# Both layers' embedding projections in the norm of the first block, none at the end of differential attention

## The chip, the cores and the metric

One NeuronCore of a Trainium2 chip runs one program. The metric is the time of one execution on the device, in microseconds (us). The engines are TensorE (PE, matrix products and transposes), VectorE (DVE), ScalarE (ACT), GpSimd (POOL) and SyncE (SP, which here only issues DMAs). Each runs its own instructions in its own order and waits on semaphores for the others.

## What is computed

One sequence of 256 tokens of width 1024 goes through a first block and then through two layers of a second block. All arithmetic is float32. Cut to what matters:

```
x  = layer_norm(ALPHA*x + g1 * token_mixer(modulate(x)))      # first block
ff = (silu(h @ w_gate) * (h @ w_up)) @ w_down
x  = layer_norm(ALPHA*x + g2 * ff, ln2_g, ln2_b)              # the norm that ends it
for i in (0, 1):                                              # second block
    h = h + mixer_i(rms_norm(h))          # 0: gated linear attention, 1: differential attention
    h = h + swiglu_2(rms_norm(h))
    gate = sigmoid(rms_norm(h, ple_norm[i]) @ ple_w_gate[i])
    h = h + gate * (p[i] @ ple_w_proj[i])                     # p[i]: 256 x 256, an input
```

The embedding projection of layer i is p[i] @ ple_w_proj[i], 256 x 256 times 256 x 1024. It depends on nothing but inputs, so it may be computed anywhere before the last line of its layer.

## The kernel before

The 256 tokens are two tiles (t = 0, 1) of 128. A product in float32 is made of three: weights and activations are each split into a rounded part (wh, xh, hh, ph) and a rest (wl, xl, hl, pl), and mm3 (L157) issues wh times xh, wl times xh and wh times xl. Weights are loaded by SP into staging tiles (st, 11 buffers) and split by gran (L141): ScalarE casts wh (L150), VectorE subtracts to get wl (L151), into tiles of wp with five buffers each. Activations are split the same way after they have been transposed on TensorE.

PSUM has eight banks: four under the tag mm (the results of projections and some transposes), four under acc (accumulators of the long products and other transposes). The program is written in Tile: the Python code issues instructions in program order, a scheduler then orders each engine's instructions, earlier code first and later code where an engine would stand, and adds the semaphores. A tile whose tag has n buffers waits until an earlier user of a buffer is done.

Block 1 ends with ffn (L803) and norm_pair (L794): norm_tile (L773) adds the residual on VectorE, squares on ScalarE (jk, L785), takes the power on GpSimd, scales x on ScalarE (L791), transposes it on TensorE and makes hT (L197), xh (L177) and xl (L178) of it, half a tile at a time. Behind it comes gla (L922), whose first projection (proj, L224) reads w_gla in four granules of 256 rows and, at its end, calls later: normed (L798) on GpSimd, two operations of 128 x 1024 for each tile (L799, L800).

ple(i, wk) (L870) is the embedding projection. For each t it loads p[i] into pr (two buffers), transposes it into an mm bank, and splits it into ph (L880) and pl (L881), each of one buffer; it splits two rows of weights; then for each t it issues 12 matmuls into two mm banks and copies them to pp (L892). Before the change ple(0) stands ahead of norm_pair in block 1, and ple(1) near the end of diff (L1144), with steps of the attention handed to it as between.

In diff the projections of q, k and v are made in six parts (parts, L1251) of 512 columns. Steps of the attention stand between their granules: heads (sc_, L1187) makes the scores of two heads for one t, the maxima (L1196), the exponentials (L1202) and the difference of both softmaxes (L1209); heads_t (at_, L1213) transposes it; out_of (L1224) multiplies by v and norms; out_t (L1245) transposes and splits the result into gt. out_rows(kb) (L1285) splits a row of the output weights and issues 12 matmuls for it; finish (L238) issues the last four rows.

The rest of what the change touches: Arow and e of attn_p (L636) in block 1 share the tag Ae with two buffers in pool b1a; bcp has two buffers under bc, which bcast (L275) fills with l1g, l1b, l2g and l2b. bias2 (L318) holds a row of biases for g2_part (L728).

Of the kernel before, what the change touches and what calls it, by code (L numbers as in the profile page):

```python
# [10 lines left out]
F32 = mybir.dt.float32  # L11
# [8 lines left out]
D = 1024  # L20
DFF = 2816
P = 128
# [60 lines left out]
def body(ctx, tc, d, out, dbg=None):  # L83
    nc = tc.nc
    V, A, T, G, Y = nc.vector, nc.scalar, nc.tensor, nc.gpsimd, nc.sync
# [7 lines left out]
    bcp = ctx.enter_context(tc.tile_pool(name="bcp", bufs=2))  # L93
# [8 lines left out]
    def mm():  # L102
        return psp.tile([P, 512], F32, name="mmb", tag="mm")
# [185 lines left out]
    def block1(adp):  # L289
        with ExitStack() as es:  # L290
# [24 lines left out]

            bias = adp.tile([P, 512], F32, name="bias")
            G.memset(bias, 0.0)
            bias2 = adp.tile([P, D], F32, name="bias2")  # L318
            G.memset(bias2, 0.0)
            wada = d["w_ada"][0]  # L320

# [27 lines left out]
                r = rstd_of(ss, 8, 1.0 / 64, EPS)  # L349
                V.tensor_tensor(v3(y, 64), v3(y, 64), head_b(r, 8, 64), op=OP.mult)  # L350

            Arow = [at_.tile([P, 1024], F32, name=f"A{t}", tag="Ae", bufs=2) for t in range(2)]
            vv = [at_.tile([P, 64], F32, name=f"vv{t}") for t in range(2)]
            u = [ap_.tile([P, 512], F32, name=f"u{t}", tag="ug", bufs=4) for t in range(2)]
            gb = [ap_.tile([P, 512], F32, name=f"gb{t}", tag="ug", bufs=4) for t in range(2)]
# [280 lines left out]
            def attn_p(t, g):  # L636
                nk = (t + 1) * P
                ts_ = slice(t * P, (t + 1) * P)
                if g == 0:
                    l8s[t] = sm.tile([P, 8], F32, name="l8", tag="l8")  # L640
                e = at_.tile([P, 4, nk], F32, name="e", tag="Ae" if t else "e0", bufs=2)
                bs = [ac(), ac()]
                for i in range(2):
                    for par, b in enumerate(bs):
                        T.matmul(b[:, i * S:i * S + nk], qT[par * 64:par * 64 + 64, 2 * g + i, ts_],
                                 kT[par * 64:par * 64 + 64, :nk], start=True, stop=False)
                    for b in bs:
                        T.matmul(b[:, i * S:i * S + nk], identr, masks[t][:, :nk], start=False, stop=True)
                for par, b in enumerate(bs):
                    bv = v3(b, S)[:, :, :nk]  # L650
                    mx = sm.tile([P, 2], F32, name="mx", tag="mx")
                    V.reduce_max(mx, bv, axis=AX.X)
                    V.tensor_scalar(mx, mx, -0.125, None, op0=OP.mult)
                    for i in range(2):
                        h = 2 * (2 * g + i) + par
                        A.activation(e[:, 2 * par + i, :], bv[:, i, :], AF.Exp, bias=mx[:, i:i + 1],
                                     scale=0.125, accum_out=l8s[t][:, h:h + 1])
                return e
# [67 lines left out]
            l1b = bcast(d["ln1_b"][0], D)  # L726

            def g2_part(hf):  # L728
                Y.dma_start(bias2[0:1, hf * 512:hf * 512 + 512], d["b_ada"][0:1, 5 * D + hf * 512:5 * D + hf * 512 + 512])
                bk, part, _ = ada_mm(ada_stage(((5 * D + hf * 512, 512),)), ac)  # L730
                V.tensor_add(part, bk, bias2[:, hf * 512:hf * 512 + 512])
                return bk, part

            def g2_row(hf, bk, part):
# [11 lines left out]
            hx = XT()  # L746
# [6 lines left out]
        with tc.tile_pool(name="f1", bufs=1) as wk:  # L753
            acc = ffn(gate_up([(d["w_gate"][0], 0), (d["w_up"][0], 0)]), d["w_down"][0], hx, None, wk,
                      {1: lambda: normed(V, l1g, l1b, 0), 3: lambda: normed(V, l1g, l1b, 1)})
            hx = XT()
            l2g = bcast(d["ln2_g"][0], D)
            l2b = bcast(d["ln2_b"][0], D)
            pp = ple(0, wk)
            gb2 = rsp.tile([P, 32], F32, name="gb2", tag="gb2", bufs=1)  # L760
            V.tensor_mul(gb2[:, 0:8], L2G, MIXG[0])
            V.tensor_mul(gb2[:, 8:16], L2B, MIXG[0])
            norm_pair(acc, g2row, gb2[:, 0:8], gb2[:, 8:16], hx, wk, ac)
            rs = [rsp.tile([P, 1], F32, name="rsx", tag="rsx") for t in range(2)]

            def later(junk):
                for t in range(2):
                    normed(G, l2g, l2b, t)
                for t in range(2):
                    rms_of(t, junk, rs[t])  # L770
            return hx, rs, later, pp

    def norm_tile(t, acc, grow, scale, shift, xt, wk, bank):  # L773
        jk = wk.tile([P, D], F32, name="jk", tag="jk", bufs=1)
# [19 lines left out]
    def norm_pair(*args):  # L794
        for t in range(2):
            norm_tile(t, *args)
# [70 lines left out]
        return r  # L867


    def ple(i, wk, between={}):  # L870
        pt = []
        for t in range(2):
            pr = wk.tile([P, 256], F32, name="pr", tag="pr", bufs=2)
            Y.dma_start(pr, d["p_2"][i, 0, t * P:(t + 1) * P, :])
            tp = mm()
            for k in range(2):
                tr(tp[:, k * P:(k + 1) * P], pr[:, k * P:(k + 1) * P])
            h = wk.tile([P, 2, P], F32R, name="ph", tag="ph", bufs=1)
            l = wk.tile([P, 2, P], F32R, name="pl", tag="pl", bufs=1)
            A.copy(h, v3(tp[:, :256], P))  # L880
            V.tensor_sub(l, v3(tp[:, :256], P), h.bitcast(F32))  # L881
            pt.append((h, l))
        pp = [ppp.tile([P, D], F32, name=f"pp{t}", bufs=1) for t in range(2)]
        gr = [row_gran(d["ple_w_proj_2"][i], k) for k in range(2)]
        for t in range(2):
            bk = [mm(), mm()]
            for k in range(2):
                wh, wl = gr[k]
                mm3(bk, pt[t][0][:, k, :], pt[t][1][:, k, :], [wh[:, :512], wh[:, 512:]], [wl[:, :512], wl[:, 512:]],
                    k == 0, k == 1)  # L890
            for n in range(2):
                A.copy(pp[t][:, n * 512:(n + 1) * 512], bk[n])  # L892
            for f in between.get(t, ()):
                f()
        return pp

    def ple_gate(i, xt, rs, pp, wk):
# [18 lines left out]

    ppp = ctx.enter_context(tc.tile_pool(name="ppp", bufs=1))
    with tc.tile_pool(name="adp", bufs=1) as adp:
        hx, rs, later, pp = block1(adp)


    def gla(xt, rs, wk):  # L922
# [185 lines left out]
    def tail_layer(i, acc, pp, nxt):  # L1108
        with tc.tile_pool(name=f"tl{i}", bufs=1) as wk:
            junk = wk.tile([P, D], F32, name="junk")  # L1110
            hx = XT()
            for t in range(2):
                residual_rms(t, acc, FFNG[i], hx, ac)
            rs = [rms_of(t, junk) for t in range(2)]
            for t in range(2):
                dump(f"mix{i}", x[t], t)
            acc = ffn(gate_up([(d["ffn_w_in_2"][i], 0), (d["ffn_w_in_2"][i], DFF)]), d["ffn_w_out_2"][i], hx, rs, wk,
                      {3: lambda: diff_consts(wk)} if nxt else {})
            hx = XT()
            for t in range(2):  # L1120
                residual_rms(t, acc, PLEG[i], hx, mm)
            rs = [rms_of(t, junk) for t in range(2)]
            for t in range(2):
                dump(f"ffn{i}", x[t], t)
            fin = ple_gate(i, hx, rs, pp, wk)
            if nxt:
                hx = XT()
                for t in range(2):
                    for n in range(2):
                        fin(t, n)  # L1130
                        hx.put_gain(t, n, blocks_t(x[t][:, n * 512:n * 512 + 512], ac), MIXG[1])
                for t in range(2):
                    dump(f"ple{i}", x[t], t)
                return hx, [rms_of(t, junk) for t in range(2)]
            for t in range(2):
                for n in range(2):
                    hs = slice(n * 512, n * 512 + 512)
                    fin(t, n)
                    Y.dma_start(out[0, t * P:(t + 1) * P, hs], x[t][:, hs])

    hx, rs = tail_layer(0, acc, pp, True)


    def diff(xt, rs, wk):  # L1144
# [121 lines left out]
        def at_(hp, t):  # L1266
            heads_t(hp, t, es[hp, t])

        def c(f, *a):
            return lambda: f(*a)  # L1270
# [6 lines left out]
                                2: [c(at_, 1, 0)], 3: [c(at_, 1, 1)]})  # L1277
        parts(1536, qk("k", 1), {0: [c(out_of, 0, 0)], 1: [c(qk_t, "q", 1, 0), c(out_of, 0, 1)], 2: [c(qk_t, "q", 1, 1)]})
        parts(2560, v_of(1), {0: [c(out_t, 0, 0)], 1: [c(qk_t, "k", 1, 0), c(out_t, 0, 1)],
                              2: [c(qk_t, "k", 1, 1)], 3: [c(sc_, 2, 0), c(sc_, 2, 1)]})  # L1280
        pp = ple(1, wk, {0: [c(at_, 2, 0), c(sc_, 3, 0)], 1: [c(at_, 2, 1), c(sc_, 3, 1)]})
        acc = accs(mm)
        wo, late = d["diff_w_out_2"][0], []

        def out_rows(kb):  # L1285
            wh, wl = row_gran(wo, kb)
            for t in range(2):
                both(acc[t], *gt(kb, t), wh, wl, kb == 0, False)

        at_(3, 0)  # L1290
        out_rows(0)
        at_(3, 1)
        out_of(1, 0)
        out_rows(1)
        out_of(1, 1)
        out_rows(2)
        out_t(1, 0)
        out_rows(3)
        out_t(1, 1)
        for kb in range(4, 8):  # L1300
            late.append((lambda t, kb=kb: gt(kb, t), *row_gran(wo, kb), False))
        finish(acc, late)
        return acc, pp

    ctx3 = tc.tile_pool(name="difw", bufs=1)
    wk = ctx3.__enter__()
    acc, pp = diff(hx, rs, wk)
    ctx3.__exit__(None, None, None)
    tail_layer(1, acc, pp, False)


_INS = ["x", "c", "w_ada", "b_ada", "w_in", "conv_w", "attn_norm_g", "conv_norm_g", "w_out", "ln1_g", "ln1_b",
# [23 lines left out]
```

## Time and profile before

| | us |
|---|---|
| median of 3 runs | 1066.44 (1065.1 to 1066.7) |
| the profiled execution | 1059.51 |
| its span, first to last instruction | 1057.7 |
| TensorE busy in the span | 1014.9 |
| VectorE busy | 631.4 |
| ScalarE busy | 560.5 |
| GpSimd busy | 56.3 |

The profile is one execution. All times below are us from the start of its span. A busy engine is one with an instruction under way; TensorE's matmuls overlap one another, so their spacing says more than their durations. The granted clock is a share of full speed: 1.00 is 2.4 GHz, and 0.5 is 1.2 GHz; a stretch with a value between has some of each. The mean over the span is 0.991.

### The profile page before, as it was taken

The page shows a single profiled execution, that of the slowest core. Times are in us where ns is not written, and L with a number is a line of the kernel's source. Part 1 is how long each engine was busy: PE and PEld are TensorE (multiplying, and loading weights), DVE is VectorE, ACT ScalarE, POOL GpSimd, SP SyncE. Part 2 cuts the span into 40 slices and gives each one's busy share as a digit, 9 for nine tenths or more (in the row PEclk, how much of TensorE's full clock was granted, in tenths as well). Part 3 has the DMA queues.
Part 4 walks back from the last instruction along what each step waited for, and adds up shares of the span by engine and source line. Part 5 has one row for each costly group of instructions (what it writes and reads, how often), then busy time and mean ns, then how long its engine had stood idle before and what let it go on. Part 6 is the DMA issues. An engine that isn't in the chain of part 4 may idle for free.

```text
span 1057.7 us, 13558 instructions
## 1 busy us (share of the span) xinstructions
PE 1014.9 (96%) x4883; PEld 810.6 (77%) x4883; DVE 631.4 (60%) x1021; ACT 560.5 (53%) x910; POOL 56.3 (5%) x47
## 2 busy tenths in 40 slices
PE   6899998999999999999999999999998999999998
PEld 3676675888888778887788888887777778888886
DVE  2378468555556466567554547578786655555654
ACT  2355448444454568465544446566857554444643
POOL 0000100000000130000000000004020100000000
PEclk9999999999999999999999999999999999999999
DMA  9958577866666155255666657535433365666601
GB/s 301 386 200 308 202 276 263 273 195 185 193 196 198 50 175 186 81 166 156 194 190 180 192 187 266 147 127 171 135 120 111 124 187 191 186 190 187 239 1 40
DMA packets 131640, 194.48 MB, mean 184 GB/s; under 512 B 10562, under 2 KB 93390, under 8 KB 131572
## 3 DMA queue, kind: packets, MB, share of 16 engines
q1 hardware_dynamic: 130792, 193.21, 57.0%
q8 instruction: 38, 0.62, 0.2%
q10 hardware_dynamic: 780, 0.40, 0.1%
q14 instruction: 30, 0.25, 0.1%
HBM read 192.53 MB, written 1.05 MB: 183 GB/s over the span
## 4 chain that ended last, share of the span: by engine, by line
PE 79%; DVE 8%; ACT 6%; DMA 2%; issue 2%; POOL 1%; SPq 0%; ACTq 0%; DVEq 0%; POOLq 0%
PE mmb L162 16%; PE mmb L159 16%; PE mmb L160 16%; PE acb L162 7%; PE acb L159 7%; PE acb L160 7%; DVE wl L151 2%; PE mmb L124 2%; ACT wh L150 1%; PE acb L124 1%; POOL rs L272 1%; ACT e L1202 1%; DMA st<-in_w_ada_dram 1%; PE mmb L333 1%; PE acb L333 1%
## 5 line engine op out<-in xcount | busy, mean ns | idle before, releaser
L151 DVE TENSOR_TENSOR wl<-st,wh 128x1024 fp32r<-128x1024 f32 (+4 forms) x292 | 350.9, 1207 | 240.1 <-ACT wh L150 237.2
L150 ACT CAST wh<-st 128x1024 fp32r<-128x1024 f32 (+4 forms) x292 | 300.6, 1038 | 280.6 <-PE mmb L162 143.6
L159 PE MATMUL mmb<-wh,xh 128*128 128x512 f32 (+4 forms) x888 | 353.4, 399 | 6.3 <-ACT xh L386 4.5
L160 PE MATMUL mmb<-wl,xh 128*128 128x512 f32 (+4 forms) x888 | 346.8, 391 | 2.1 <-DVE wl L151 2.1
L162 PE MATMUL mmb<-wh,xl 128*128 128x512 f32 (+4 forms) x888 | 342.8, 391 | 6.0 <-DVE xl L178 4.7
L159 PEld LDWEIGHTS mmb<-wh,xh 128*128 128x128 f32 x888 | 169.1, 191 | 44.7 <-ACT xh L386 6.3
L162 PEld LDWEIGHTS mmb<-wh,xl 128*128 128x128 f32 x888 | 169.1, 190 | 44.5 <-DVE xl L178 6.3
L160 PEld LDWEIGHTS mmb<-wl,xh 128*128 128x128 f32 x888 | 169.3, 191 | 33.3 <-DVE wl L151 2.8
L159 PE MATMUL acb<-wh,hh 128*128 128x512 f32 x216 | 84.0, 389 | 0.0
L160 PE MATMUL acb<-wl,hh 128*128 128x512 f32 x216 | 84.0, 389 | 0.0
L162 PE MATMUL acb<-wh,hl 128*128 128x512 f32 x216 | 66.6, 389 | 0.0
L159 PEld LDWEIGHTS acb<-wh,hh 128*128 128x128 f32 x216 | 40.6, 188 | 8.4
L162 PEld LDWEIGHTS acb<-wh,hl 128*128 128x128 f32 x216 | 40.5, 188 | 8.4
L160 PEld LDWEIGHTS acb<-wl,hh 128*128 128x128 f32 x216 | 40.5, 188 | 8.4
L866 POOL TENSOR_TENSOR rsx<-rsx,mhalf 128x1 f32<-128x1 f32 x12 | 10.2, 851 | 468.2 <-DVE rsx L865 468.2
L272 POOL TENSOR_TENSOR rs<-rs,mhalf 128x8 f32<-128x8 f32 (+1 forms) x14 | 20.0, 1433 | 241.1 <-DVE rs L271 241.1
L836 ACT ACTIVATE sg<-mmb,rsx 128x256 f32<-128x256 f32 x44 | 20.7, 474 | 22.2 <-PE mmb L162 20.4
L151 DVE TENSOR_TENSOR wxl<-st,wxh 128x1024 fp32r<-128x1024 f32 x22 | 26.7, 1219 | 3.1 <-ACT wxh L150 3.1
L837 DVE SCALAR_TENSOR_TENSOR sg<-mmb,rsx,sg 128x256 f32<-128x256 f32 x44 | 20.8, 480 | 11.1 <-ACT sg L836 11.1
L150 ACT CAST wxh<-st 128x1024 fp32r<-128x1024 f32 x22 | 22.7, 1052 | 5.1 <-PE acb L162 3.0
L124 PE MATMUL mmb<-ident,sg 128*128 128x128 f32 x132 | 21.1, 275 | 2.7 <-DVE sg L837 2.1
L843 DVE TENSOR_TENSOR hl<-mmb,hh 128x512 fp32r<-128x512 f32 x33 | 22.6, 685 | 1.8 <-ACT hh L842 1.8
(311 smaller groups left out, 1062.7 us busy)
## 6 DMA issues: line engine op xcount, KB each, us to landing
st<-in_ffn_w_in_dram SPq DMA_DIRECT2D x176, 256.0 KB
st<-in_ffn_w_out_dram SPq DMA_DIRECT2D x44, 512.0 KB
st<-in_w_ada_dram SPq DMA_DIRECT2D x32, 512.0 KB
st<-in_diff_w_in_dram SPq DMA_DIRECT2D x24, 512.0 KB
st<-in_w_gate_dram SPq DMA_DIRECT2D x44, 256.0 KB
st<-in_w_up_dram SPq DMA_DIRECT2D x44, 256.0 KB
st<-in_w_down_dram SPq DMA_DIRECT2D x22, 512.0 KB
st<-in_w_ada_dram SPq DMA_DIRECT2D x32, 256.0 KB
```

Of the source, the lines that this page charges most:

```text
L124: T.transpose(o, i, ident)
L150: A.copy(h[:, :n], src)
L151: V.tensor_sub(l[:, :n], src, h[:, :n].bitcast(F32))
L159: T.matmul(p_, xh, wh, start=start, stop=False)
L160: T.matmul(p_, xh, wl, start=False, stop=False)
L162: T.matmul(p_, xl, wh, start=False, stop=stop)
L272: G.tensor_tensor(r[:, :n], r[:, :n], mhalf[:, :n], op=OP.pow)
L333: T.matmul(bk[32 * j:32 * j + 32, :n], cB[:, kb, :], sts[kb // k][:, kb % k * n:kb % k * n + n], start=kb < 4, stop=kb >= 4)
L836: A.activation(sg, ps[t][:, 0:256], AF.Silu, scale=rs[t])
L837: V.scalar_tensor_tensor(sg, ps[t][:, 256:512], rs[t], sg, op0=OP.mult, op1=OP.mult)
L843: V.tensor_sub(hl, tv, hh.bitcast(F32))
L1202: A.activation(es_[:, i, :], b[:, i * S:(i + 1) * S], AF.Exp, bias=mx[:, i:i + 1], scale=rh[:, i:i + 1], accum_out=L[t][:, s, 2 * hp + i:2 ...
```

## The change

ple(1) is called in block 1, right after norm_pair, and the results of both layers are kept to their use: pp has four tiles where it had two. In diff nothing stands in the place of ple(1); the steps of the attention that it carried are written out between the output rows, in a new order, and sc(2, 0) moves one granule up. The parameter between of ple goes. In SBUF, bias2 is halved (the first half of g2's bias uses bias), and Arow and the second tile's e take their two buffers from bcp under the tag bc, where the broadcast rows of the layer norms are.

```diff
-            bias2 = adp.tile([P, D], F32, name="bias2")
+            bias2 = adp.tile([P, 512], F32, name="bias2")
...
-            Arow = [at_.tile([P, 1024], F32, name=f"A{t}", tag="Ae", bufs=2) for t in range(2)]
+            Arow = [bcp.tile([P, 1024], F32, name=f"A{t}", tag="bc") for t in range(2)]
...
-                e = at_.tile([P, 4, nk], F32, name="e", tag="Ae" if t else "e0", bufs=2)
+                e = bcp.tile([P, 4, nk], F32, name="e", tag="bc") if t else at_.tile([P, 4, nk], F32, name="e", tag="e0", bufs=2)
...
-                Y.dma_start(bias2[0:1, hf * 512:hf * 512 + 512], d["b_ada"][0:1, 5 * D + hf * 512:5 * D + hf * 512 + 512])
+                Y.dma_start(bias2[0:1, :] if hf else bias[0:1, :], d["b_ada"][0:1, 5 * D + hf * 512:5 * D + hf * 512 + 512])
                 bk, part, _ = ada_mm(ada_stage(((5 * D + hf * 512, 512),)), ac)
-                V.tensor_add(part, bk, bias2[:, hf * 512:hf * 512 + 512])
+                V.tensor_add(part, bk, bias2 if hf else bias)
...
-            pp = ple(0, wk)
+            pps = [ple(0, wk)]
...
             norm_pair(acc, g2row, gb2[:, 0:8], gb2[:, 8:16], hx, wk, ac)
+            pps.append(ple(1, wk))
...
-    def ple(i, wk, between={}):
+    def ple(i, wk):
+        bank = mm
...
-        pp = [ppp.tile([P, D], F32, name=f"pp{t}", bufs=1) for t in range(2)]
+        pp = [ppp.tile([P, D], F32, name=f"pp{i}{t}", bufs=1) for t in range(2)]
...
-            for f in between.get(t, ()):
-                f()
...
         parts(2560, v_of(1), {0: [c(out_t, 0, 0)], 1: [c(qk_t, "k", 1, 0), c(out_t, 0, 1)],
-                              2: [c(qk_t, "k", 1, 1)], 3: [c(sc_, 2, 0), c(sc_, 2, 1)]})
-        pp = ple(1, wk, {0: [c(at_, 2, 0), c(sc_, 3, 0)], 1: [c(at_, 2, 1), c(sc_, 3, 1)]})
+                              2: [c(qk_t, "k", 1, 1), c(sc_, 2, 0)], 3: [c(sc_, 2, 1)]})
...
+        at_(2, 0)
+        sc_(3, 0)
+        out_rows(0)
+        at_(2, 1)
+        sc_(3, 1)
+        out_rows(1)
         at_(3, 0)
-        out_rows(0)
+        out_rows(2)
+        out_of(1, 0)
         at_(3, 1)
-        out_of(1, 0)
-        out_rows(1)
         out_of(1, 1)
-        out_rows(2)
+        out_rows(3)
         out_t(1, 0)
-        out_rows(3)
         out_t(1, 1)
...
-    tail_layer(1, acc, pp, False)
+    tail_layer(1, acc, pps[1], False)
```

## Rows read from the trace of the kernel before

**Rows 1.** Page, part 1: busy us, share of the span, instructions.
```profile
PE 1014.9 (96%) x4883; PEld 810.6 (77%) x4883; DVE 631.4 (60%) x1021; ACT 560.5 (53%) x910; POOL 56.3 (5%) x47
```

**Rows 2.** Page, part 4: the chain that ended last, shares by engine.
```profile
PE 79%; DVE 8%; ACT 6%; DMA 2%; issue 2%; POOL 1%; SPq 0%; ACTq 0%; DVEq 0%; POOLq 0%
```

**Rows 3.** Stretches, differential attention: length, busy PE, PEld, DVE, ACT, POOL, clock, DMA share, GB/s.
```profile
743.00:765.00 22.00, 20.50 (x103) 15.45 (x103) 16.64 (x43) 18.92 (x46) 0.00 (x0) 1.00 0.32 100
...
795.00:800.00 5.00, 3.00 (x17) 2.12 (x15) 4.55 (x13) 3.55 (x13) 0.00 (x0) 0.95 0.72 222
800.00:803.30 3.30, 3.30 (x13) 2.47 (x11) 1.59 (x6) 2.89 (x9) 0.00 (x0) 0.56 0.00 0
```

**Rows 4.** Order of time, PE, ple(1): start, us, instruction, [idle before, releaser].
```profile
795.56 0.66 PE L124 MATMUL mmb<-ident,pr 128*128 128x128 f32 x4
798.22 0.50 PE L159 MATMUL mmb<-wh,ph 128*128 128x512 f32 x1 [2.00 <-ACT ph L880]
798.55 0.39 PE L160 MATMUL mmb<-wl,ph 128*128 128x512 f32 x1
798.78 0.40 PE L159 MATMUL mmb<-wh,ph 128*128 128x512 f32 x1
...
800.29 0.63 PE L160 MATMUL mmb<-wl,ph 128*128 128x512 f32 x1
800.72 0.63 PE L159 MATMUL mmb<-wh,ph 128*128 128x512 f32 x1
```

**Rows 5.** Order of time, PE, the norm that ends block 1.
```profile
365.45 0.62 PE L162 MATMUL mmb<-wh,pl 128*128 128x512 f32 x2
...
367.52 0.46 PE L159 MATMUL mmb<-wh,xh 128*128 128x416 f32 x1 [0.68 <-ACT xh L177]
...
369.50 0.71 PE L162 MATMUL mmb<-wh,xl 128*128 128x416 f32 x1 [1.33 <-DVE xl L178]
...
372.43 0.55 PE L160 MATMUL mmb<-wl,xh 128*128 128x416 f32 x1
...
373.20 0.35 PE L160 MATMUL mmb<-wl,xh 128*128 128x416 f32 x1
373.39 0.35 PE L162 MATMUL mmb<-wh,xl 128*128 128x416 f32 x1
...
380.94 0.46 PE L162 MATMUL mmb<-wh,xl 128*128 128x416 f32 x1 [1.90 <-DVE xl L178]
```

**Rows 6.** Stretches, the norm: columns as in the first such group.
```profile
370.00:374.00 4.00, 4.00 (x16) 3.84 (x15) 2.79 (x3) 3.55 (x7) 1.67 (x1) 0.64 0.02 6
```

**Rows 7.** Groups of instructions, 793.5 to 827: line, operation, count, busy us, mean ns.
```profile
L892 ACT COPY pp<-mmb 128x512 f32<-128x512 f32 x4 | 2.1, 594 | 0.0
...
L881 DVE TENSOR_TENSOR pl<-mmb,ph 128x256 fp32r<-128x256 f32 x2 | 0.8, 420 | 0.8 <-PE mmb L162 0.8
```

**Rows 8.** Order of time, ACT, the norm.
```profile
372.65 0.90 ACT L150 CAST wh<-st 128x832 fp32r<-128x832 f32 x1
```

**Rows 9.** Tile xl, 350 to 385 (ns min/median/max), and POOL in order of time.
```profile
L178 DVE TENSOR_TENSOR xl<-hT,xh x4: 691/1815/2857, 367.5 to 378.0; 128x512 fp32r<-128x512 f32 x4
...
377.36 2.97 POOL L800 TENSOR_TENSOR x<-x,bc 128x1024 f32<-128x1024 f32 x1
```

**Rows 10.** Tile bc: count, ns min/median/max, first and last start in us.
```profile
L277 SPq DMA_DIRECT2D bc<-in_ln_b_dram x2: 465/539/613, 95.9 to 197.5; - x2
L799 DVE TENSOR_TENSOR x<-x,bc x2: 1217/1221/1225, 166.1 to 173.7; 128x1024 f32<-128x1024 f32 x2
```

**Rows 11.** Order of time, PE, the last transposes of block 1's e.
```profile
121.19 1.09 PE L124 MATMUL acb<-ident,e 128*128 128x128 f32 x8
```

**Rows 12.** Stretches, block 1: columns as in the first such group.
```profile
60.00:66.00 6.00, 6.00 (x32) 5.32 (x32) 5.50 (x20) 5.34 (x9) 0.00 (x0) 1.00 0.86 302
...
156.00:162.00 6.00, 6.00 (x35) 4.27 (x37) 3.87 (x12) 2.73 (x5) 1.00 (x1) 1.00 0.00 1
```

**Rows 13.** Waits of SP, 330 to 390: total us, times, longest.
```profile
SPq L130 <- DVE wl L151: 48.8, 11, 24.9
```

More of the change, by code (lines that the diff above doesn't have):

```diff
@@ L770, in later @@
                     rms_of(t, junk, rs[t])
-            return hx, rs, later, pp
+            return hx, rs, later, pps
     def norm_tile(t, acc, grow, scale, shift, xt, wk, bank):
@@ L874, in ple @@
             Y.dma_start(pr, d["p_2"][i, 0, t * P:(t + 1) * P, :])
-            tp = mm()
+            tp = bank()
             for k in range(2):
@@ L882, in ple @@
             pt.append((h, l))
-        pp = [ppp.tile([P, D], F32, name=f"pp{t}", bufs=1) for t in range(2)]
+        pp = [ppp.tile([P, D], F32, name=f"pp{i}{t}", bufs=1) for t in range(2)]
         gr = [row_gran(d["ple_w_proj_2"][i], k) for k in range(2)]
         for t in range(2):
-            bk = [mm(), mm()]
+            bk = [bank(), bank()]
             for k in range(2):
@@ L918, in body @@
     with tc.tile_pool(name="adp", bufs=1) as adp:
-        hx, rs, later, pp = block1(adp)
+        hx, rs, later, pps = block1(adp)
     def gla(xt, rs, wk):
@@ L1139, in tail_layer @@
                     Y.dma_start(out[0, t * P:(t + 1) * P, hs], x[t][:, hs])
-    hx, rs = tail_layer(0, acc, pp, True)
+    hx, rs = tail_layer(0, acc, pps[0], True)
     def diff(xt, rs, wk):
@@ L1302, in diff @@
         finish(acc, late)
-        return acc, pp
+        return acc
     ctx3 = tc.tile_pool(name="difw", bufs=1)
     wk = ctx3.__enter__()
-    acc, pp = diff(hx, rs, wk)
+    acc = diff(hx, rs, wk)
     ctx3.__exit__(None, None, None)
-    tail_layer(1, acc, pp, False)
+    tail_layer(1, acc, pps[1], False)
 _INS = ["x", "c", "w_ada", "b_ada", "w_in", "conv_w", "attn_norm_g", "conv_norm_g", "w_out", "ln1_g", "ln1_b",
```

## The prediction

> **What bounds the kernel now.** I read the page first: TensorE is busy 96% of the span [rows 1], and 79% of the chain that ended last is TensorE's [rows 2]. Matrix work sets the time, so a change pays only where TensorE waits or runs at its low clock. No instruction on TensorE is added or dropped here: one projection of 24 matmuls, ple(1), moves from the end of differential attention to the norm that ends block 1. What counts is how much waiting it leaves behind and how much it fills.
>
> So I read two stretches by the view of stretches, then by the order of time. At the end of differential attention, in 795 to 800 us TensorE is busy 3.00 of 5 us and in 800 to 803.3 its granted clock is 0.56 [rows 3]. The order of time names the cause: ple(1)'s first matmul waited 2.00 us for ph, ScalarE's cast, and some 2 us later the same matmuls start 0.43 us apart (800.29, 800.72) instead of 0.23 (798.55, 798.78) [rows 4]: the 1.2 GHz level after a gap in 2.4 GHz work. The projection meant as cover for the softmax stands in ScalarE's queue between the exponentials and is itself late.
>
> In the norm, with ple(0) already there, TensorE waits 0.68 us for xh, 1.33 us for xl and later 1.90 us for the last xl [rows 5], and from 370 to 374 the clock is 0.64 [rows 6], which costs 4 x 0.36 = 1.4 us. Together 5.3 us could be filled.
>
> **What leaves differential attention.** 24 matmuls x 0.23 = 5.5 us and four transposes, some 0.6 us (0.66 for the row of four) [rows 4]: 6.1 us of TensorE. With them go the 2.00 us wait for ph [rows 4] and the low clock, 3.3 x 0.44 = 1.5 us [rows 3]. That is 9.6 us. Off ScalarE go four pp copies (2.1 us) and two ph casts, off VectorE two pl (0.8 us) [rows 7], besides the weight splits of two rows.
>
> What comes back is softmax without that cover. Out_rows(0) to (3), 12 matmuls or 2.8 us each, now stand one behind each sc/at step, and sc(2,0) starts inside the last projection. The same chain of four head steps runs in the first half under other projections: from 743 to 765 TensorE is idle 22.00 - 20.50 = 1.5 us [rows 3]. I take 1.5 us, because that row has the same instructions on ScalarE and VectorE. The bounds are 0 (all covered) and 1.5 + 2.0 + 1.5 = 5.0 us (the wait and the low clock return elsewhere). At the very end out_t(1,0) has out_of(1,1) and one out_rows in front of it where it had out_of(1,1) and one and a half; that small loss is in the 1.5. Gain: 9.6 - 1.5 = 8.1 us, between 4.6 and 9.6.
>
> **What the norm pays.** It receives the 6.1 us. If all 5.3 us of waits were filled, it would pay 0.8 us. I don't expect that, for three reasons. First, the scheduler gives each engine what comes first in the program, and later work only where an engine would stand. ple(1) is written behind norm_pair. In the norm ScalarE is the full engine: the first instruction on it that belongs to work behind the norm is a weight cast at 372.65 [rows 8]. Second, ph has one buffer, held until ple(0)'s last matmul (365.45 + 0.62) [rows 5], so ple(1)'s ph can't be cast in the earlier quiet time; I put it in the place of that weight cast, near 372.7. Third, wh has five buffers. Before, ple(0)'s two rows and three granules of gla's first projection were split ahead; now it is four ple rows and one granule. Eleven gla matmuls started from 367.52 to 372.43 [rows 5]; with one granule and only the first token tile ready there are six. The five that are missing cost 5 x 0.19 = 1.0 us (spacing 373.20 to 373.39 [rows 5]).
>
> So the waits of 0.68 and 1.33 us and the low clock stay; ple(1)'s 24 matmuls come after 372.7 and cover the 1.90 us wait for xl; ph of the second tile waits for the first tile's matmuls, for which I set 0.4 us (bounds 0 and the 2.00 of [rows 4], taken near the low end since ScalarE has no exponentials in this stretch). Cost: 6.1 + 1.0 - 1.9 + 0.4 = 5.6 us. The bounds are 0.8 us (all filled) and 8.9 us (the slower rival below).
>
> VectorE's part has a hazard. xl takes 0.69 us alone and up to 2.86 us in this stretch, while GpSimd's normed runs (2.97 us from 377.36) [rows 9]. pl is 0.42 us [rows 7] but none stands beside GpSimd in this trace; bounds 0.42 and 1.7 us (four times, as for xl). I take 0.42, pl's own row; the other end, 2 x 1.3 = 2.6 us, is inside the 8.9.
>
> The Trainium skill (SBUF — State Buffer, Who interferes with whom) says that a VectorE instruction with two SBUF inputs is held until a GpSimd instruction that reads SBUF is done, and one with a single SBUF input is not. The trace agrees for xl, which has two: the GpSimd instruction of 377.36 ends at 380.33 and the wait on xl ends at 380.94. By that rule pl, which reads PSUM, keeps 0.42 and the norm pays 5.6; by the xl row it would pay 8.2.
>
> **The edits that make room.** Arow and the second tile's e move from a pool of their own into bc, with the same two buffers in the same turn, so nothing among them changes. But l1g and l1b now wait for e. l1b was issued at 95.9 us [rows 10]; it will now be issued behind the second e's transposes at 121.19 [rows 11]. Queued behind both on SP are the last w_ada tiles and the w_out rows. The cover is that the DMA engines drain before the data is short: share 0.00 from 156 to 162 [rows 12], and l1g is first used at 166.1 [rows 10]. I cost it at nothing; if that cover were gone it would cost the two transfers of 512 KB, 3.5 us at the 302 GB/s of 60 to 66 [rows 12]. The halved bias2 costs nothing: g2_part(0) reuses bias long after its last reader. p_2 of layer 1 waits on SP for the pr buffers until ple(0)'s transposes; behind it on SP are gla's weight tiles, but SP stands there for up to 24.9 us anyway, for a stage buffer that VectorE's wl frees [rows 13].
>
> **Sum.** -8.1 + 5.6 = -2.5 us on a span of 1057.7, so 1055.2; with the 1.8 us around the span (the profiled execution is 1059.5), 1057.0. The median of the runs is 6.9 us above the profiled execution; I carry that over: 1066.4 - 2.5 = 1063.9 us. With 6.8 to 9 us for the one and 4.5 to 6.5 for the other, this case runs from 1061.9 to 1066.1.
>
> **Rivals.**
> The norm takes all of it. If ScalarE has an earlier gap for ph, the 24 matmuls fill 367 to 373 and the clock doesn't fall: 0.8 us paid, -7.3, 1059.1. For: 5.3 us of waits are there. Against: the single ph buffer and ScalarE full to 372.65 [rows 5, 8].
> Softmax is bare. The wait and the low clock return in front of at(2,0) or out_t(1,0): gain 4.6, so +1.0, 1067.4, which can't be told from no change. For: ScalarE's exponentials set the pace there. Against: the 1.5 us of the first half [rows 3].
> Slower: gla is shut out of PSUM. If the mm banks go round in program order, gla's first banks are those of ple(1)'s first tile, and none of the eleven matmuls starts before ple(1) has been copied out: 11 x 0.19 = 2.1 us lost instead of 1.0. It decides from the point at which gla's first matmul comes after ple(1)'s first pp copy. The wait for xl then isn't covered but only moved: 6.1 + 2.1 + 0.4 = 8.6, and 0.3 for the longer spell at low clock, 8.9 us. Against a gain halfway between 4.6 and 8.1, 6.4, this is +2.5, 1068.9. For: six mm banks are asked for by each ple, and there are four. Against: a scheduler that hands out whichever bank is free.
>
> **How the numbers follow.** Chances: forecast 0.52, norm takes all 0.13, softmax bare 0.17, shut out of PSUM 0.18. A measurement of this kernel can tell about 0.2%, 2.1 us, from no change. Two thirds of the forecast's case lie beyond that (0.34), with 0.13 of the first rival: faster 0.47. A third of the forecast (0.18), most of bare softmax (0.15) and 0.03 of the last: same 0.36. The rest: slower 0.17. The range goes from 1059.0, which takes in the first rival's time, to 1069.0, which takes in the last one's; what lies beyond both is under 2 in 10.
>
> **What would show it.** Right: no ph at the end of differential attention, that stretch without a clock of 0.56, and finish there some 8 us earlier after the start of the last projection; in the norm a ph near 373, the waits of 0.68 and 1.33 still there, and gla's first projection ending 5 to 6 us later. Wrong: ph before 370; gla's first matmul behind a pp copy of ple(1); a new wait of 2 us on e, od or xl among out_rows; or a shift of more than 1 us before 350, which I hold to be nothing.

## The result, and the profile after

The changed kernel is slower. In eight runs it took 1076.65 us (median; 1068.4 to 1078.3), in eight beside them the kernel before took 1065.95: a ratio of 1.0093 with a 95% interval of 1.007 to 1.0116, some 10 us. Run again later it gave 1.0087 (1.0056 to 1.0119). The profiled execution took 1076.23 us, with a span of 1074.4. TensorE's first line on the page now reads (busy us, share, instructions; before: [rows 1]):

```profile
PE 1024.4 (95%) x4883; PEld 815.6 (76%) x4883; DVE 634.7 (59%) x1021; ACT 562.0 (52%) x910; POOL 56.9 (5%) x47
```

The instructions are as many as before; TensorE is busy 9.5 us longer and idle 50.0 us where it was 42.8. To see where, I took the start of the same instruction in both traces and noted how much later it comes. Each column of this table is the growth of that shift over one stretch of the kernel, against the profiled execution of before; the other kernels belong to the experiments further down. That execution of before took 1059.51 us, some 6 us under the median of its runs, so the columns between say more than the last one.

| kernel | up to norm 1 | norm 1 | second norm, and gla | diff | end |
|---|---|---|---|---|---|
| changed | +5.1 | +5.3 | +13.3 | -7.0 | +16.7 |
| changed, run again (e6) | +1.2 | +5.4 | +9.3 | -2.6 | +13.2 |
| e1 room edits only | +0.9 | +5.4 | +0.2 | -0.4 | +6.0 |
| e5 room, ln loads in ffn | +4.6 | +1.7 | +0.1 | +0.1 | +7.3 |
| e2 room in pp | +0.4 | 0.0 | +10.3 | -5.7 | +5.0 |
| e3 e2, acc banks | +3.1 | 0.0 | +6.3 | -7.1 | +2.3 |
| e8 e3, two ph | +5.9 | 0.0 | +6.7 | -4.5 | +8.1 |
| e4 without ple(1) | +3.8 | 0.0 | +1.4 | -7.1 | -1.9 |
| e7 e2, ple(1) ahead of the norm | +5.3 | 0.0 | +6.1 | -7.1 | +4.3 |
| e9 e7, normed on VectorE | +4.9 | 0.0 | +0.7 | -5.9 | -0.3 |
| e13 before, normed on VectorE | +5.9 | 0.0 | -3.1 | -0.3 | +2.5 |
| e15 e2, normed on VectorE | +5.1 | 0.0 | +7.1 | -6.0 | +6.2 |

(Norm 1 runs from the first jk to ffn's first sg, the second norm and gla from the third jk to the next ffn's first sg, diff from the last sgm of layer 0 to the first sg behind it. Small shifts elsewhere are left out, so rows don't always add up. e10 to e12 and e14 are told of below.)

The first column is one execution beside another, not the change: TensorE's order there is the same in all of them, and the last section comes back to it. Three places are left.

**Norm 1.** Each kernel has its own line numbers. Before, ScalarE cast two wh in the midst of the norm of tile 0, and TensorE began ffn without a wait:

```profile
161.94 1.99 ACT L150 CAST wh<-st 128x1024 fp32r<-128x1024 f32 x2
...
166.30 0.79 PE L159 MATMUL mmb<-wh,xh 128*128 128x512 f32 x1
```

In the changed kernel, TensorE in order of time (start, us, instruction, [idle before, releaser]), then ScalarE, then SP:

```profile
174.46 1.36 PE L124 MATMUL acb<-ident,x 128*128 128x128 f32 x8 [1.00 <-ACT x L792]
180.56 1.22 PE L159 MATMUL mmb<-wh,xh 128*128 128x512 f32 x2 [4.75 <-ACT wh L150]
181.82 0.80 PE L160 MATMUL mmb<-wl,xh 128*128 128x512 f32 x1
...
178.89 0.67 ACT L177 CAST xh<-hT 128x512 fp32r<-128x512 f32 x1
...
179.41 4.88 ACT L150 CAST wh<-st 128x1024 fp32r<-128x1024 f32 x5
...
131.32 0.38 SPq L277 DMA_DIRECT2D bc<-in_ln_g_dram x1
131.80 0.38 SPq L277 DMA_DIRECT2D bc<-in_ln_b_dram x1
```

l1b was issued at 95.9 [rows 10]; now both loads are issued at 131, in the midst of the w_out tiles. And ScalarE does the whole norm of tile 1 before it casts ffn's first wh, all five of them at 179.41; TensorE waits 4.75 us for the first, and goes on at 1.2 GHz (granted clock 0.50 from 181.8 to 184.6, 0.63 us a matmul).

**The second norm.** TensorE, VectorE, GpSimd, ScalarE (the row that answers [rows 8] is ph at 383.11, in that cast's place):

```profile
377.14 0.60 PE L124 MATMUL mmb<-ident,pr 128*128 128x128 f32 x4
382.77 1.11 PE L124 MATMUL acb<-ident,x 128*128 128x128 f32 x4 [5.03 <-ACT x L792]
383.55 0.79 PE L159 MATMUL mmb<-wh,ph 128*128 128x512 f32 x1
...
391.39 0.73 PE L162 MATMUL mmb<-wh,pl 128*128 128x512 f32 x2 [2.42 <-DVE pl L883]
...
393.67 0.55 PE L159 MATMUL mmb<-wh,xh 128*128 128x416 f32 x1
...
383.86 0.42 DVE L883 TENSOR_TENSOR pl<-mmb,ph 128x256 fp32r<-128x256 f32 x1
384.31 6.09 DVE L151 TENSOR_TENSOR wl<-st,wh 128x832 fp32r<-128x832 f32 x2
390.32 0.68 DVE L178 TENSOR_TENSOR xl<-hT,xh 128x512 fp32r<-128x512 f32 x1
390.93 0.41 DVE L883 TENSOR_TENSOR pl<-mmb,ph 128x256 fp32r<-128x256 f32 x1
...
384.02 2.38 POOL L800 TENSOR_TENSOR x<-x,bc 128x1024 f32<-128x1024 f32 x1 [1.92 <-PE acb L124]
386.48 3.04 POOL L801 TENSOR_TENSOR x<-x,bc 128x1024 f32<-128x1024 f32 x1
...
383.11 0.39 ACT L882 CAST ph<-mmb 128x256 fp32r<-128x256 f32 x1
...
387.59 1.08 ACT L894 COPY pp<-mmb 128x512 f32<-128x512 f32 x2
```

gla's first matmul stood at 367.52 [rows 5]; it now stands at 393.67, behind all 24 of ple(1) and behind their first pp copy. The matmuls of gla that used to stand among the waits are gone from there, so TensorE runs dry for 5.03 us until the last half of x comes. Later ple(1) itself waits 2.42 us: its pl takes 0.41 us, but stands on VectorE behind two wl that took 6.09 us while GpSimd's normed ran. 7.5 us of waits have taken the place of 3.9.

**Differential attention**, as a whole, before and after (stretch: length, busy PE, PEld, DVE, ACT, POOL, clock, DMA share, GB/s), then TensorE's waits there after (total, times, longest):

```profile
743.00:856.00 113.00, 104.80 (x535) 82.77 (x535) 81.31 (x163) 78.20 (x181) 13.50 (x10) 0.98 0.40 124
```

```profile
766.70:872.75 106.05, 99.21 (x507) 76.97 (x507) 77.94 (x159) 73.98 (x173) 13.53 (x10) 1.00 0.41 124
```

```profile
PE acb L124 <- DVE r L1173: 1.6, 2, 1.3
PE acb L124 <- ACT e L1202: 1.5, 1, 1.5
PE acb L124 <- DVE od L1242: 1.3, 1, 1.3
```

28 instructions fewer, 7.0 us shorter, no stretch below full clock in this execution, and no wait for ph. The waits for r and e are those of before; the one for od was 0.6 us. The low clock isn't gone for good, though. Of the thirteen profiled executions with the new order of diff (all rows of the table that have it, and e10 to e12 and e14), six have no 1.2 GHz stretch in diff and are 7.0 to 7.4 us shorter than before. Seven have one, first of all just behind the old wait of 1.5 us for e in the first half. Five of these are 5.6 to 6.1 us shorter, e8 4.5, and the changed kernel's own second execution (e6) 2.6, with two stretches:

```profile
768.10:774.90 6.80, 6.80 (x22) 4.79 (x24) 3.55 (x9) 3.79 (x8) 0.00 (x0) 0.50 0.20 49
839.70:843.10 3.40, 3.40 (x9) 2.62 (x8) 1.64 (x3) 0.68 (x1) 0.00 (x0) 0.51 0.48 154
```

### The profile page after: what moved, and what is told of

It is laid out like the page before. It is cut to its first block, busy times and chain, and to the rows that moved or that the text cites. A ratio compares the mean times of both kernels' runs of the same rounds, so it can differ in the third digit from the quotient of the medians.

```text
span 1074.4 us, 13565 instructions
## 1 busy us (share of the span) xinstructions
PE 1024.4 (95%) x4883; PEld 815.6 (76%) x4883; DVE 634.7 (59%) x1021; ACT 562.0 (52%) x910; POOL 56.9 (5%) x47
## 4 chain that ended last, share of the span: by engine, by line
PE 81%; DVE 7%; ACT 6%; DMA 3%; issue 2%; POOL 1%; SPq 0%; ACTq 0%; DVEq 0%; POOLq 0%
PE mmb L159 17%; PE mmb L162 17%; PE mmb L160 16%; PE acb L162 7%; PE acb L159 7%; PE acb L160 7%; PE mmb L124 2%; DVE wl L151 2%; ACT wh L150 1%; PE acb L124 1%; POOL rs L272 1%; PE acb L333 1%; PE mmb L333 1%; DMA st<-in_w_ada_dram 1%; DMA ggk<-in_diff_g_k_dram 1%
## 5 line engine op out<-in xcount | busy, mean ns | idle before, releaser
L151 DVE TENSOR_TENSOR wl<-st,wh 128x1024 fp32r<-128x1024 f32 (+3 forms) x292 | 355.1, 1221 | 245.4 <-ACT wh L150 243.5
L150 ACT CAST wh<-st 128x1024 fp32r<-128x1024 f32 (+3 forms) x292 | 301.1, 1038 | 294.2 <-PE mmb L162 159.9
L863 ACT ACTIVATE junk<-x 128x1024 f32<-128x1024 f32 x10 | 10.6, 1060 | 26.8 <-DVE x L856 25.2
```

Source lines behind the costliest of these rows:

```text
L150: A.copy(h[:, :n], src)
L151: V.tensor_sub(l[:, :n], src, h[:, :n].bitcast(F32))
L863: A.activation(junk, x[t], AF.Square, accum_out=ss)
```

## Experiments: the room

**e1.** The kernel before with the three room edits and nothing else (the diff's lines on bias2, Arow and e).

> The kernel before with only the edits that make room: Arow and the second tile's e in bc, bias2 halved. ple(1) stays in differential attention. Theory A, read from the trace of the changed kernel: l1g and l1b are loaded only once e has left bc, SP stands there ahead of the w_out and w_ada tiles, and the scheduler, which then has ffn's first weights later, writes the norm of tile 1 ahead of their casts; a wait of 4 to 5 us for wh in front of ffn's first matmul, and 5 us slower than before: about 1071. Rival B: norm 1 changed because of ple(1), not because of the room; no such wait, within 1 us of before, about 1066. Rival C: the room also costs the shift of 3.5 us that the changed kernel shows ahead of 66 us: about 1074.

1069.09 us, ratio 1.0046 (1.0022 to 1.007): 4.9 us. Norm 1 is that of the changed kernel, to the wait (TensorE):

```profile
176.29 1.22 PE L159 MATMUL mmb<-wh,xh 128*128 128x512 f32 x2 [4.75 <-ACT wh L150]
```

Theory A. C fell: the shift ahead of 66 us is not there. The halved bias2 isn't the cause: e2 below keeps it, and its norm 1 costs nothing.

**e5.** e1, and both loads go behind ffn's first weight tiles:

```diff
-            l1g = bcast(d["ln1_g"][0], D)
-            l1b = bcast(d["ln1_b"][0], D)
...
-                      {1: lambda: normed(V, l1g, l1b, 0), ...
+                      {0: ln1, 1: lambda: normed(V, *l1, 0), ...      # ln1 makes both loads
```

> As e1 (the kernel before with the room edits), but l1g and l1b are loaded inside ffn, behind its first eight weight tiles on SP. They still wait for e. Theory A: what costs e1 its 5 us in norm 1 is that both loads stand on SP ahead of ffn's first weights, by which the scheduler counts on these later and writes the casts of wh behind the norm of tile 1; with the loads behind them ffn's first matmul comes within 1 us of its place before, no wait of 4 us for wh, and the time is that of before, 1064 to 1065. Rival B: the wait for e itself, or the place of Arow and e in memory, is the cause: 1069, as e1.

1066.93 us, 1.0031 (1.0007 to 1.0054), between A and B. The order is as it was: the wh are cast at 166.58 and ffn's first matmul comes 9.8 us after the first jk (8.7 before, 17.8 in e1). So the place of the two loads on SP decides where the casts are written, with e in bc all the same. But there is a new wait: normed now waits for l1g and stands ahead of a wl (TensorE, then VectorE).

```profile
172.00 0.79 PE L159 MATMUL mmb<-wh,xh 128*128 128x512 f32 x1
...
180.01 0.50 PE L160 MATMUL mmb<-wl,xh 128*128 128x512 f32 x1 [4.02 <-DVE wl L151]
...
175.15 1.23 DVE L802 TENSOR_TENSOR x<-x,bc 128x1024 f32<-128x1024 f32 x1 [3.16 <-DMA bc<-in_ln_g_dram]
```

So the time doesn't come all the way back, for a reason of this kernel's own. Why the planned order goes by these loads (that it counts on ffn's weights later) is argued; that it does is shown.

**e2.** The changed kernel, with Arow and e in the two pp tiles of ple(1):

```diff
-            Arow = [bcp.tile([P, 1024], F32, name=f"A{t}", tag="bc") for t in range(2)]
+            Arow = [ppp.tile([P, 1024], F32, name=f"A{t}", tag=f"pp1{t}", bufs=1) for t in range(2)]
...
-                e = bcp.tile([P, 4, nk], F32, name="e", tag="bc") if t else ...
+                e = ppp.tile([P, 4, nk], F32, name="e", tag=f"pp1{g}", bufs=1) if t else ...
```

> The changed kernel, but Arow and the second tile's e take their buffers from the two pp tiles of ple(1), which nothing else uses before 380 us, so that l1g and l1b don't wait. ple(1) stays in the norm. Theory A: norm 1 goes as before, its 5 us come back, and the norm that ends block 1 still pays 13: 1076.7 - 5, about 1071 to 1072. Rival B: the room is not the cause; 1076. Rival C: it also held the shift ahead of 66 us: 1068.

1065.36 us, 1.0014 (0.9997 to 1.0032). Norm 1 costs 0.0, the second norm 10.3: theory A's places. The time lies below all three, nearest to C's. 1.0046 and 1.0014 make 1.006, the changed kernel 1.0093.

**e6.** The changed kernel again.

> The changed kernel again. Theory A: its loss is the sum of e1 (+0.46%) and e2 (+0.14%): 1.006, about 1070.5, with as many 1.2 GHz stretches as those two have (four to six in the span). Rival B: it keeps the 1.0093 of its first runs, about 1074, with two to four stretches at 1.2 GHz more than e1 and e2: then the two losses aren't merely added. In the profile, by A and B: a shift of 5 us in norm 1 and of 10 to 13 in the norm that ends block 1; the shift ahead of 66 us comes or goes from run to run.

1072.88 us, 1.0087 (1.0056 to 1.0119). Against the sum of e1 and e2, 6.4 us, this is 9.3; the intervals of both allow 4 more. Whether the two losses help each other isn't settled.

## Experiments: the norm

**e4.** ple(1) left out altogether, without the room edits; diff in the changed order. Its time is that of the diff side alone.

> ple(1) is left out altogether: layer 1 uses layer 0's projection, and the room edits are undone. Differential attention is in the changed order. What is left is the gain of the diff side alone. By the shifts of the two traces between the first scores of the second half and the last sigmoid (23.7 to 16.7 us) it is 7.0: about 1059. The prediction's 8.1 would give 1058; bare softmax (4.6) would give 1061.5. No 1.2 GHz stretch and no wait over 1 us among out_rows by the first two; a wait of 2 us or a clock of 0.56 there by the last.

1057.7 us, 0.9947 (0.9927 to 0.9967): 5.6 us less than before, by the trace 7.1, and no low clock in diff. The interval, 3.5 to 7.8 us, takes in bare softmax's 4.6 and not the prediction's 8.1; by its trace, which has no low clock and no wait over 1.5 us in diff, it isn't bare. Taken with e2 (1.0014), ple(1) in the norm costs 0.67%, 7.1 us; the intervals leave some 3 us either way, so that this is more than the 6.1 us of its own TensorE work isn't shown by the times.

**e3.** e2, and ple(1) takes acc banks: `bank = ac if i else mm`.

> As e2, and ple(1) takes its six PSUM banks under the tag acc instead of mm. ph, pl and the five wh buffers are as they were. Theory A (gla is shut out of PSUM): gla's first matmuls stand ahead of ple(1) again and fill the waits for xh and xl; of the 13 us of the norm some 5 stay: 8 us under e2, about 1063 to 1064. Rival B (the five wh buffers, which hold four rows of ple, shut gla out): order and time as e2, about 1071. Rival C: the acc banks make x's transposes wait for ple(1)'s copies, a new wait of 2 to 4 us: 1066 to 1068.

The order is A's: gla's first granule, six matmuls, is back ahead of ple(1) and its waits for xh and xl are those of before; a wait of 1.80 us for x is new, where before waited 1.90 for the last xl:

```profile
370.60 0.46 PE L159 MATMUL mmb<-wh,xh 128*128 128x416 f32 x1 [0.69 <-ACT xh L177]
...
372.57 0.46 PE L162 MATMUL mmb<-wh,xl 128*128 128x416 f32 x1 [1.32 <-DVE xl L178]
...
375.39 1.12 PE L124 MATMUL acb<-ident,x 128*128 128x128 f32 x4 [1.80 <-ACT x L792]
...
380.94 0.40 PE L159 MATMUL acb<-wh,ph 128*128 128x512 f32 x1
```

The five wh buffers (B) therefore didn't keep gla out; the banks did. The stretch is 4.0 us shorter than in e2, but the median isn't: 1065.87, 1.001 (0.9988 to 1.0032). A's 8 us under e2 didn't come. So of the banks the mechanism is shown, and its worth by time is not.

**e8.** e3, with two buffers for ph.

> As e3 (ple(1) in acc banks), and ph has two buffers, so that the casts of ple(1) no longer wait for the last matmuls of the tile before. Theory A (the single ph is a small cost, as predicted, 0.4 us): within 1 us of e3, 1065 to 1066. Rival B (the single ph is what keeps ple(1) out of the early waits): ple(1)'s matmuls start some 4 us earlier against the norm, and the time is 2 to 4 us under e3, 1062 to 1064.

1063.02 us, 0.9999 (0.9977 to 1.0021); the stretch +6.7 against +6.3. ScalarE's second ph, in e3 and in e8:

```profile
383.45 0.37 ACT L882 CAST ph<-acb 128x256 fp32r<-128x256 f32 x1 [3.06 <-PE acb L160]
```

```profile
383.55 0.40 ACT L882 CAST ph<-acb 128x256 fp32r<-128x256 f32 x1
```

It no longer waits, and counted from the norm's first jk it comes 2.7 us earlier; ple(1)'s first matmul does not (0.7 us later). So the single ph costs little, as A says. The time as such is B's, but by the ratios it is 1.1 us under e3, which the intervals can't tell from none.

**e7.** e2, and `pps = [ple(0, wk), ple(1, wk)]` ahead of norm_pair.

> As e2 (no cost in norm 1), but ple(1) is called ahead of norm_pair, right behind ple(0). Theory A: what e2 pays in the norm, 10.3 us in its profile, is that ple(1) stands behind norm_pair in the program and so is ready for TensorE only once the waits for x are over; ahead of it, its 24 matmuls stand in the 5.0 us wait for x, and the norm and gla pay 4 to 6: 4 to 5 us under e2, about 1060 to 1061. Rival B: ScalarE decides; the second ph cast and four pp copies (2.9 us) ahead of the second tile's x and hT put the norm off by as much, and the time stays within 1.5 us of e2, 1064 to 1066.

1063.44 us, 0.9995 (0.9971 to 1.0018): 2 us under e2, not 4 to 5. The wait for x is gone, the norm costs 6.1 instead of 10.3, but a wait for wl has come:

```profile
386.82 0.71 PE L160 MATMUL mmb<-wl,xh 128*128 128x416 f32 x1 [2.58 <-DVE wl L151]
```

**e9.** e7, and in later `normed(V, l2g, l2b, t)` for `normed(G, ...)`.

> As e7, but the four operations of normed behind the norm run on VectorE instead of GpSimd. In e7 the wait for x is gone and 3.3 us of waits for wl came in its place, while GpSimd's normed ran beside VectorE's wl. Theory A: GpSimd's normed holds wl up (two wl together took 6.09 us in the changed kernel where one takes 1.03); without it each wl takes 0.9 to 1.1 us, the wait for wl goes, and the time is 2 to 3 us under e7, about 1061. Rival B: VectorE then carries 4 x 1.22 = 4.9 us more ahead of the wl, so that the wait stays or grows: e7 or up to 2 us more, 1063 to 1066.

1055.7 us, 0.9911 (0.9885 to 0.9937): 8 us under e7 and 10 under before, the best of all. VectorE and GpSimd in e7:

```profile
372.54 0.42 DVE L882 TENSOR_TENSOR pl<-mmb,ph 128x256 fp32r<-128x256 f32 x1 [3.36 <-ACT ph L881]
...
383.58 3.19 DVE L151 TENSOR_TENSOR wl<-st,wh 128x832 fp32r<-128x832 f32 x1 [3.08 <-ACT wh L150]
...
372.25 2.40 POOL L799 TENSOR_TENSOR x<-x,bc 128x1024 f32<-128x1024 f32 x1 [3.61 <-ACT pp L893]
...
383.52 2.36 POOL L800 TENSOR_TENSOR x<-x,bc 128x1024 f32<-128x1024 f32 x1
```

and VectorE in e9:

```profile
380.60 1.22 DVE L800 TENSOR_TENSOR x<-x,bc 128x1024 f32<-128x1024 f32 x1
381.90 1.03 DVE L151 TENSOR_TENSOR wl<-st,wh 128x832 fp32r<-128x832 f32 x1
```

The same wl takes 3.19 us beside GpSimd's normed and 1.03 without it, and normed itself takes 1.22 on VectorE for 2.4 to 3.0 on GpSimd. The wait for wl falls from 2.58 (not 3.3, as the expectation has it) to 0.41. Theory A's mechanism, but some three times its 2 to 3 us. Second norm and gla in e7, then in e9 (columns as in the stretches above):

```profile
360.33:517.65 157.32, 149.92 (x740) 123.01 (x738) 96.42 (x176) 101.00 (x170) 16.74 (x14) 0.98 0.45 142
```

```profile
359.97:511.85 151.88, 147.52 (x740) 120.32 (x738) 96.25 (x180) 100.76 (x170) 6.84 (x10) 1.00 0.47 147
```

Of 5.4 us, TensorE's idle time is 3.0; the other 2.4 are busy time, and e7 has two 1.2 GHz stretches there where e9 has none. The medians show 2 to 3 us more than these two executions; that isn't explained.

**e13, e15, e14.** Is that a gain of its own? normed on VectorE in the kernel before (e13), in e2 (e15) and in the changed kernel (e14).

> The kernel before with one edit: normed behind the norm on VectorE. Theory A: what GpSimd's normed costs before is the waits for xl of 1.33 and 1.90 us and some of the 1.2 GHz stretch behind them, 2 to 4 us: ratio 0.996 to 0.998, about 1062; e9's 0.9911 then holds 5 us that come from where ple(1) stands and from the end of differential attention. Rival B: it is worth 8 us here too, 0.991 to 0.992; then the move of ple(1) gives nothing even in its best place.

> e2 with normed on VectorE: ple(1) behind norm_pair in mm banks, no cost in norm 1. Theory A (GpSimd's hold is the larger part of the norm's cost): 5 us or more under e2, ratio 0.995 to 0.997, that is close to e13 + 0 to 2 us. Rival B (that ple(1) stands ahead of gla is the larger part): 2 us under e2 at most, 0.9995 to 1.0005.

> The changed kernel with normed on VectorE. The wait of 2.2 to 2.4 us for pl goes (pl stood behind two wl that took 6.09 us); the wait of 5.0 us for x goes or shrinks as xl no longer holds ScalarE's hT. Theory A: 4 to 6 us under the changed kernel, ratio 1.003 to 1.005, norm 1 keeps its 5 us. Rival B: 1 to 2 us, 1.007, if the order of ple(1) ahead of gla is the whole cost.

e13: 1061.34 us, 0.9967 (0.9944 to 0.9989), theory A by the time: 3.5 us of it the kernel before could have too. Of the two waits for xl only the second, 1.90, goes; the first stays at 1.41, now behind normed's own 2 x 1.22 us on VectorE. e15: 1063.86, 1.0002 (0.998 to 1.0025), theory B: only 1.3 us under e2. Its TensorE:

```profile
374.70 0.66 PE L124 MATMUL acb<-ident,x 128*128 128x128 f32 x4 [2.36 <-ACT x L792]
378.80 0.80 PE L159 MATMUL mmb<-wh,ph 128*128 128x512 f32 x1 [3.43 <-ACT ph L882]
```

With normed out of the way the wait for x shrinks to 2.36, and the next one comes, 3.43 for ph, which ScalarE casts where the program has it, behind the norm; gla is still shut out behind ple(1). e14: 1070.35, 1.0064 (1.0039 to 1.0089), 2.4 us under the changed kernel, nearer to B; norm 1 keeps its 5.3. So neither repair does much alone (e7 2 us, e15 1.3), and both together bring 11, by the ratios, from e2 to e9: with ple(1) behind the norm, ph and the banks are the next limit; with normed on GpSimd, wl is.

**e11, e12, e10.** Other places: ple(1) near the end of gla, or in the tail behind it, both without room edits (its pp in a pool opened after block 1); and e8 with normed on VectorE.

> No room edits and nothing in the norm: ple(1) is called near the end of gla, ahead of the output projection, its pp in a pool of its own that is opened behind block 1; differential attention in the changed order. TensorE waits for only 1.8 us there (wl at 483 us of the kernel before). Theory A: ple(1) costs what its TensorE work is, 6.1, less what of the wait it fills: 4.3 to 6.1; from e4's 0.9947, about 1062 to 1063.8. Rival B: its casts and copies put the last gates and the output projection off, 1065 or more.

> As e11, but ple(1) is called in the layer's tail, ahead of the residual that follows gla, in acc banks, where TensorE has waits of 1.8 us ahead and under 0.5 us behind and then 20 us of transposes and first ffn weights. Theory A: 4.3 to 6.1 us over e4, 1062 to 1064, as e11. Rival B: in acc banks it stands in the way of x's transposes: 1065 or more.

> As e8 (ple(1) behind norm_pair, acc banks, two ph), with normed on VectorE. Theory A: the waits for xl (3.1 us in e8) shrink to under 1 us since no GpSimd work holds xl up; 2 to 3 us under e8, about 1060 to 1061. Rival B: normed on VectorE stands ahead of xl or wl and costs what it saves; 1063, as e8.

1059.99 (0.996, 0.9939 to 0.998), 1061.71 (0.9953, 0.9934 to 0.9971) and 1060.66 (0.995, 0.993 to 0.997). In gla and in the tail ple(1) costs its work less a little by the trace (+4.1, +4.7), near what their theories A say, and norm 1 costs nothing: 4 to 5 us better than before, and the simplest. By the ratios they are only 1.4 and 0.6 us over e4, where 4.3 to 6.1 was expected; the intervals don't settle which holds. e10 meets its theory A: of the waits for xl, 3.1 us in e8, 0.4 stay.

## Why the prediction was wrong

The forecast was 2.5 us faster than before, 1063.9 us; it came out 9 to 11 us slower than before, beyond the range. Two steps failed: the room was put at nothing, and six matmuls of gla were taken to stay ahead of ple(1). The gain in diff was put somewhat too high besides.

- **Diff, -8.1 predicted: -7.0 to -7.4 by the traces without a low clock in diff, -2.6 to -6.1 by those with one, -5.6 by e4's ratio.** Right in kind. The wait for ph went; the low clock went from its place, and in seven of thirteen executions came back in another. In the first profile TensorE's idle time fell by 1.4 us (113.00 - 104.80 against 106.05 - 99.21), not 0.5: of the 1.5 us that softmax without its cover was to cost, some 0.6 came, among it a wait for od of 1.3 us where it was 0.6. Its busy time fell by 5.6, not 7.6; that term was too large, and which part of it is open. "Softmax is bare" fell as to the wait, which didn't return; its low clock did, in some executions.
- **Room, 0 predicted: +5.3 by the trace, 4.9 by e1.** The step that failed is the cover. I asked whether the loads would land in time, and they did. What they changed is where ScalarE's casts of wh are written in the order, which no DMA share can show. My price for lost cover, 3.5 us, was that of two transfers; the real price was the norm of a whole tile standing ahead of five casts. I named the shift of more than 1 us ahead of 350 as a sign of error: it came, but as a sign it is poor, since e4, without the room edits and with TensorE's order unchanged up to there, has +3.8 too.
- **The norm, +5.6 predicted: +9.3 and +13.3 by the traces, 7.1 by e2 and e4 (some 3 us either way).** ph came where I put it, 383.11 for 372.7 and a shift of 10.5. But gla's first matmul came behind ple(1)'s first pp copy (393.67 against 387.59), the point from which "gla is shut out of PSUM" decides; I gave that 0.18, against it only that a scheduler might hand out whichever bank is free. It doesn't: e3, which changes only the tag of the banks, puts six matmuls of gla ahead again, the six I had counted. By the traces even that rival's 8.9 was too small (9.3 to 13.3), because I moved 2.1 us of gla's matmuls and forgot that with them gone nothing covers the wait for x: 5.03 us. With the order I had assumed (e3, e8) the stretch costs 6.3 and 6.7, near my 5.6, but not term by term: in e3 TensorE's idle time there stays as before where I had 1.5 us less, and its busy time grows by 6.3 where I had 7.1.
- **pl beside GpSimd.** The Trainium skill (SBUF — State Buffer, Who interferes with whom) says that a VectorE instruction with one SBUF input doesn't wait for GpSimd's, and one with two does. The traces agree with both halves: pl took 0.42 us in the midst of normed (e7, 372.54), wl 3.19 instead of 1.03. My choice for pl was right and beside the point: pl is in time only if what stands ahead of it on VectorE is, and that were two wl, with two SBUF inputs each.
- **"Norm takes all of it".** The 0.8 us of that rival is what e9 pays (0.7), but only with ple(1) ahead of norm_pair and normed off GpSimd; neither was in the change. And normed off GpSimd shortens the same stretch by 3.1 in the kernel before (e13), so there ple(1) itself costs 3.8. By the ratios it costs nothing that can be told: e4 and e13 together make 0.9914, e9 0.9911.

The two misses add up: 4.9 (room) and 1.5 (norm 7.1, diff -5.6) are 6.4 by the separate kernels, and 9.3 to 10.7 were measured.

## What to carry to other kernels

Moving work into a hole of TensorE brings little unless it is ready there and stands in the right order: look at which bank, which cast and which VectorE instruction it will stand behind, and at what it pushes out of the hole. An edit that only makes room can change the order in which engines are given their work, far from where it stands; take buffers from something idle for the whole time, as e2 did, and compare the orders. Work put on GpSimd because it is idle can still cost time through what it holds up on VectorE: here 3.5 us in the kernel before.

## What the runs showed of the hardware

TensorE's clock makes executions of the same order differ by nearly as much as the change itself. Stretch from the start to norm 1, with TensorE's order the same in both, in e12 and in e8 (columns as above, clock behind POOL):

```profile
0.00:157.00 157.00, 140.04 (x786) 98.13 (x787) 89.56 (x236) 69.12 (x140) 8.22 (x11) 0.99 0.80 282
```

```profile
0.00:157.00 157.00, 140.18 (x756) 97.86 (x757) 86.76 (x228) 68.65 (x139) 7.79 (x11) 0.93 0.78 275
```

At 0.99 the kernel reaches norm 1 0.8 us earlier than before's execution, at 0.93 5.9 us later; the shift of 3.5 us ahead of 66 us in the changed kernel, which a rival of e1 held to be the room's, is of this kind. Over the runs of the kernel before, the mean granted clock goes from 0.981 (1070.3 us) to 0.994 (1059.5); the changed kernel's first runs have 0.989 in two (1068.4 and 1069.0) and 0.977 to 0.983 in six (1076.2 to 1078.3). At the same mean clock, 0.989, three runs of the changed kernel lie at 1068.4 to 1069.0 and eight of before at 1061.5 to 1064.6, means 5.6 us apart; what the medians show beyond that, some 3 to 5 us, goes with a lower clock. That its waits bring more stretches at 1.2 GHz would fit both this and the 3 to 4 us by which its loss exceeds the sum of e1 and e2, but no run here shows it; nor do they tell why a gap brings such a stretch in one execution and not in another.
